# A hybrid encoder step: the second norm's product without GpSimd, the first FFN tiles feature by feature

## The chip, the cores and the metric

The kernel runs on one core of a Trainium2 chip. Such a core has five engines that work side by side, each through its own instructions in order: TensorE (PE, matmuls; PEld is its loading of weights), VectorE (DVE), ScalarE (ACT), GpSimd (POOL) and SyncE (SP, which here issues DMAs). The metric is the device time of one execution in microseconds, of the slowest core, here the only one. The kernel before takes 1071.52 us, the median of 3 runs (1070.22 to 1071.63).

## The reference, cut to what matters

One layer is applied to 512 prompt positions and to 32 sample positions, with 1024 features and an FFN of width 2816. The first half of the layer (first norm, input projection, attention, short convolution, gated merge) isn't touched by the change. From there on, for both streams:

```python
    x = x + gate1[:, None, :] * (merged @ w_out)

    h2 = modulate(rms_norm(x, g_norm2), shift2, scale2)      # xn * (1 + scale) + shift
    up, gate = jnp.split(h2 @ w_up, 2, axis=-1)
    up_c, new_ffn = causal_dwconv(up, ffn_prev, w_fconv, b_fconv)
    x = x + gate2[:, None, :] * ((jax.nn.silu(up_c) * gate) @ w_down)
```

The norm divides each position by the root of its mean square over the 1024 features. Shift, scale and gate are vectors over the features, one set for the prompt and one for the sample.

## The kernel before, in words

**Layout.** Features lie on the 128 partitions, in 8 tiles (KD = 8); the 544 positions are columns. They are cut into two halves of 272 columns (`HALF`), each of 256 prompt and 16 sample columns. As the modulation differs between prompt and sample, an operation that uses it is issued twice per half, on 256 and on 16 columns (`streams`, L662).

**Matmuls.** Each fp32 operand is split in a rounded part and the rest (`xh`, `xl`; `wh`, `wl`), and a product is three matmuls: `wh` with `xh`, `wh` with `xl`, `wl` with `xh` (`mm3_steps`, L105). One output tile of 128 features for one half is 8 features x 3 = 24 matmuls of 272 columns. The accumulators in PSUM rotate among three (`acc`, L121).

**The stretch of the change.** `w_out` has 8 output tiles. Tiles 0 to 3 are done for both halves at once. Tiles 4 to 7 ("late") are done for the first half in `out_half(0)` and then for the second in `out_half(1)` (L711). After each, `residual` (L667) adds the gated tile into `xr` on DVE, ACT squares it, and POOL adds the squares up in `sacc` for tiles 1 to 6 (L677); tile 0's squares start `sacc`, tile 7's stay in `sq2`. `norm` (L680) sums both over the features with matmuls against ones (`ss`), and `rstd_of` (L167) makes the inverse root `rs` from it: Ln and Exp on ACT, one Newton step on DVE (L171 to L176).

`h2` (L690) then makes the input of the FFN for one half, feature by feature (k = 0 to 7): POOL multiplies `xr` by `rs` into `hf` (L694; six buffers), DVE scales and shifts it, for prompt and sample apart (L697), and `split` (L89) has ACT round it to `h2h` (L91) and DVE subtract to get `h2l` (L92). The weights of the first FFN tiles, 0, KF = 22 (the gate of 0) and 1, are loaded ahead into the pool `early`, and `up_half(i)` (L718) computes these three tiles for one half, one tile after the other. From there the loop over `f` (L742) goes on: ACT copies the up tile out of its accumulator (L747), DVE convolves it, ACT applies silu (L750), DVE multiplies with the gate's accumulator (L754), and the result is split into `fh` and `fl`, which lie in memory that `early` and the pool of `mh` and `ml` have given back.

**What sets the order.** The instructions are written in program order, and a planner orders them for each engine: of those whose inputs are ready by its own model of durations, the one written first goes first. `tc.high_priority()` puts both calls of `norm` ahead of what was written before them. `after(inst, earlier)` (L154) makes the planner put `inst` behind `earlier` on their engine. In `h2` of the first half, features 5 to 7 are put so behind the last residual of `out_half(1)`.

Of the kernel before, what the change touches and what calls it, by code (L numbers as in the profile page):

```python
# [12 lines left out]
F32 = mybir.dt.float32  # L13
F32R = mybir.dt.float32r
AF = mybir.ActivationFunctionType
ALU = mybir.AluOpType
# [34 lines left out]
def build(tc, a):  # L51
    nc = tc.nc
    ctx = ExitStack()
    with ctx:
# [34 lines left out]
        def split(hi, lo, x, eng=nc.vector):  # L89

            nc.scalar.copy(hi, x)  # L91
            eng.tensor_tensor(lo, x, hi.bitcast(F32), ALU.subtract)  # L92

        def load_w(src, nk=KD, pool=wp, hl_bufs=2, lo=nc.vector):
            raw = wp.tile([P, KD, P], F32, tag="raw", bufs=4, name="raw")
            nc.sync.dma_start(raw[:, :nk], src)
            wh = pool.tile([P, KD, P], F32R, tag="wh", bufs=hl_bufs, name="wh")
            wl = pool.tile([P, KD, P], F32R, tag="wl", bufs=hl_bufs, name="wl")
            nc.scalar.copy(wh[:, :nk], raw[:, :nk])  # L99
            lo.tensor_tensor(wl[:, :nk], raw[:, :nk], wh[:, :nk].bitcast(F32), ALU.subtract)  # L100
            return wh, wl

        HALF = ((0, HT), (HT, T))

        def mm3_steps(ps, wh, wl, xh, xl, k0=0, nk=KD, first=True, last=True, cols=HALF):  # L105
            for k in range(nk):
                for w, xs in ((wh, (xh, xl)), (wl, (xh,))):
                    for n, x in enumerate(xs):
                        s = first and k == 0 and w is wh and n == 0
                        e = last and k == nk - 1 and w is wl  # L110
                        for i, (c0, c1) in enumerate(cols):
                            nc.tensor.matmul(ps[:, i, 0:c1 - c0], w[:, k], x[:, k0 + k, c0:c1], start=s, stop=e)  # L112
                yield

        def mm3(*args, **kw):
            for _ in mm3_steps(*args, **kw):
                pass
# [3 lines left out]
        def acc():  # L121
            acc_pools.rotate(-1)
            return acc_pools[-1].tile([P, 2, 512], F32, tag="mm", name="ps")[:, :, 0:HT]

        def proj(w, x):

            if not isinstance(w, tuple):
                w = load_w(w)
            ps = acc()
            mm3(ps, *w, *x)  # L130
            return ps
# [22 lines left out]
        def after(inst, earlier):  # L154

            tc.add_manual_dep(inst.ins, earlier.ins.name,
                              mybir.DependencyInfo(mybir.DependencyClass.NoSync, mybir.DependencyReason.DATA))
# [27 lines left out]
        mods = cp.tile([P, 6, KD, 2], F32, name="mods")  # L185
# [144 lines left out]
        for k in range(KD):  # L330
# [5 lines left out]
            hf = xt[:, k]  # L336
# [4 lines left out]
        for w, slot, post in zip(ws, slots, (queries, keys)):  # L341
            ps = slot[:, :, 0:HT]
# [56 lines left out]
        def transposed(sg):  # L399

            out = []
            for g in ROWS:
                at = pz.tile([P, 512], F32, tag="z", name="at")
                c = 0
                for i in g:
                    for b in range(i + 1):
                        s0 = SEG[b] + P * (i - b)
                        nc.tensor.transpose(at[:, c + P * b:c + P * b + P], sg[:, s0:s0 + P], ident)  # L408
                    c += P * (i + 1)
                ah = sp.tile([P, 512], F32R, tag="ah", bufs=3, name="ah")  # L410
                al = sp.tile([P, 512], F32R, tag="al", bufs=3, name="al")
                split(ah[:, :c], al[:, :c], at[:, :c])
                out.append((ah, al))
            return out
# [89 lines left out]
        earlier = None  # L504
        for j in range(NP):
            for e in range(2):
# [7 lines left out]
                earlier = (j, e, transposed(sg), vt)  # L514
# [112 lines left out]
        for b, w0, wb, br in ((0, 7 * KD, "w_branch_b", (bh, bl)), (1, 6 * KD, "w_branch_a", (oh, ol))):  # L627
# [7 lines left out]
            for m in range(KD):  # L635
                ps = proj(W[w0 + m], x)
                sg = mbp.tile([P, 2, HT], F32, tag="sg", bufs=2, name="sgm")
                last = nc.scalar.activation(sg, ps, AF.Sigmoid)
                ps = proj(load_w(a[wb][m], lo=nc.gpsimd), br)
# [15 lines left out]
        xr = xp.tile([P, KD, T], F32, name="xr")  # L655
# [3 lines left out]
        rs = xp.tile([P, T], F32, name="rs")  # L659
        sq2 = xp.tile([P, T], F32, name="sq2")  # L660

        def streams(c0, c1):  # L662

            e = c0 // HT * HT + HP
            return [(n, a_, b_) for n, a_, b_ in ((0, c0, min(c1, e)), (1, max(c0, e), c1)) if a_ < b_]

        def residual(ps, s, m, c0, c1):  # L667

            for n, a_, b_ in streams(c0, c1):
                r = xr[:, m, a_:b_]  # L670
                added = nc.vector.scalar_tensor_tensor(r, ps[:, a_ - c0:b_ - c0], mods[:, s, m, n:n + 1], r,
                                                       ALU.mult, ALU.add)
            sq = sacc[:, c0:c1] if m == 0 else sq2[:, c0:c1] if m == KD - 1 else \
                xp.tile([P, HT], F32, tag="sq", bufs=2, name="sq")
            nc.scalar.activation(sq, xr[:, m, c0:c1], AF.Square)  # L675
            if 0 < m < KD - 1:
                nc.gpsimd.tensor_tensor(sacc[:, c0:c1], sacc[:, c0:c1], sq, ALU.add)  # L677
            return added
# [8 lines left out]
        h2h = hp.tile([P, KD, T], F32R, tag="hh", name="h2h")  # L687
        h2l = hp.tile([P, KD, T], F32R, tag="hl", name="h2l")

        def h2(c0, c1, earlier=None):  # L690

            for k in range(KD):
                hf = xp.tile([P, HT], F32, tag="hf", bufs=6, name="hf2")
                nc.gpsimd.tensor_tensor(hf, xr[:, k, c0:c1], rs[:, c0:c1], ALU.mult)  # L694
                for n, a_, b_ in streams(c0, c1):
                    v = hf[:, a_ - c0:b_ - c0]
                    v = nc.vector.tensor_scalar(v, v, mods[:, 4, k, n:n + 1], mods[:, 3, k, n:n + 1], ALU.mult, ALU.add)  # L697
                    if earlier and k >= 5:
                        after(v, earlier)
                split(h2h[:, k, c0:c1], h2l[:, k, c0:c1], hf)  # L700

        tables = log_tables(last)
        wo = tc.alloc_tile_pool(name="wo", bufs=1)
# [1 line left out]
        for m in range(KD - NW):  # L705
            ps = proj(a["w_out"][m], (mh, ml))
# [2 lines left out]
        late = [(m, load_w(a["w_out"][m], pool=wo, hl_bufs=NW)) for m in range(KD - NW, KD)]  # L709

        def out_half(i):  # L711
            for m, w in late:
                ps = acc()[:, 0:1]
                mm3(ps, *w, mh, ml, cols=(HALF[i],))
                done = residual(ps[:, 0], 2, m, *HALF[i])
            return done

        def up_half(i):  # L718
            for w, ps in first.values():
                mm3(ps[:, i:i + 1], *w, h2h, h2l, cols=(HALF[i],))  # L720

        out_half(0)
        done = out_half(1)
        with tc.high_priority():
            norm(*HALF[0], tables, (sq2, sacc))
        h2(*HALF[0], done)
        first = {m: (load_w(a["w_up"][m], pool=early, hl_bufs=3), acc()) for m in (0, KF, 1)}
        with tc.high_priority():
            norm(*HALF[1], tables, (sq2, sacc))
        up_half(0)  # L730
        h2(*HALF[1])
        up_half(1)
        wo.release()
        ftp = ctx.enter_context(tc.tile_pool(name="ftmp", bufs=1))
# [7 lines left out]
        for f in range(KF):  # L742
            ps = first[f][1] if f in first else proj(a["w_up"][f], (h2h, h2l))
# [7 lines left out]
            ps = first[KF][1] if f == 0 else proj(a["w_up"][KF + f], (h2h, h2l))  # L751
# [7 lines left out]
        for m in range(KD - 1):  # L759
            ps = acc()  # L760
# [8 lines left out]
        m = KD - 1  # L769
# [7 lines left out]
        for c in HALF:  # L777
            ps = acc()[:, 0:1]
# [3 lines left out]
            cs = slice(*c)  # L782
# [74 lines left out]
```

## Time and profile before

| what | value |
|---|---|
| median of 3 runs | 1071.52 us |
| the profiled execution, own time | 1071.4 us |
| its span, from the first to the last instruction | 1069.7 us |
| PE busy | 1030.6 us (96%) |
| DVE busy | 616.0 us (58%) |
| ACT busy | 387.1 us (36%) |
| POOL busy | 164.9 us (15%) |
| mean granted TensorE clock | 0.990 |

Shares of busy time are averages over the whole span. The span is the time between the first and the last instruction of the profiled execution, and the execution's own time lies 1.7 us above it. A wait in the rows is written as "idle before", with the engine, tile and line that ended it.

### The profile page before, as it was taken

To read this page: it belongs to the slowest core of one execution; us is meant where nothing else is said; L and a number is where in the kernel's file an instruction comes from. 1 tells how busy PE (TensorE), PEld (TensorE's weight loads), DVE (VectorE), ACT (ScalarE), POOL (GpSimd) and SP (SyncE) were. 2 spreads that over 40 slices of the span, in tenths; PEclk is the share of its full clock that TensorE was granted. 3 is DMA by queue.
4 is the path that set the end of the run, shared out by engine and by line. 5 is a ranking of instruction groups with operands and counts; after the bars stand their busy time and mean duration, and the time that the engine had idled before them with its cause. 6 is when DMAs were issued, how large, how long until landed. Compare 5 with 4: busy or idle time off the path is not lost.

```text
span 1069.7 us, 19270 instructions
## 1 busy us (share of the span) xinstructions
PE 1030.6 (96%) x8042; PEld 1010.9 (95%) x8042; DVE 616.0 (58%) x914; ACT 387.1 (36%) x637; POOL 164.9 (15%) x247
## 2 busy tenths in 40 slices
PE   3899999999999999999999998999999999999995
PEld 1689999999999999999999997999999999999995
DVE  6956666656675556665777569454454545422234
ACT  5455544544443332222232443332323333332231
POOL 2520000000001112112111145000010001000112
PEclk9899999999999999999999999999999999999998
DMA  9636555554213225555555650123222222332312
GB/s 372 242 87 201 147 162 137 146 141 131 60 52 106 90 77 172 178 177 178 168 178 168 222 178 1 40 80 99 80 94 85 83 95 80 91 89 78 92 50 84
DMA packets 43271, 133.44 MB, mean 125 GB/s; under 512 B 5296, under 2 KB 8496, under 8 KB 43056
## 3 DMA queue, kind: packets, MB, share of 16 engines
q1 hardware_dynamic: 43040, 132.07, 39.1%
q8 instruction: 63, 1.03, 0.4%
q14 instruction: 24, 0.20, 0.1%
q10 hardware_dynamic: 144, 0.14, 0.1%
HBM read 112.60 MB, written 6.75 MB: 112 GB/s over the span
## 4 chain that ended last, share of the span: by engine, by line
PE 91%; DVE 5%; issue 1%; DMA 1%; ACT 1%; POOL 0%; SPq 0%; DVEq 0%; ACTq 0%; POOLq 0%
PE ps L112 83%; PE o L370 2%; PE z L370 2%; PE at L408 2%; DVE hf L697 1%; DVE adum L196 1%; PE slot L112 1%; DMA cbc<-in_c_dram 1%; PE mt L315 1%; DVE h2l L92 1%; DVE xt L337 0%; SPq L289 0%; PE so L370 0%; PE tp L268 0%; POOL hl L92 0%
## 5 line engine op out<-in xcount | busy, mean ns | idle before, releaser
L99 ACT CAST wh<-raw 128x1024 fp32r<-128x1024 f32 x153 | 159.1, 1041 | 362.3 <-PE ps L112 269.0
L100 DVE TENSOR_TENSOR wl<-raw,wh 128x1024 fp32r<-128x1024 f32 (+1 forms) x133 | 161.1, 1214 | 189.8 <-ACT wh L99 189.1
L112 PE MATMUL ps<-hh,wh 128*128 128x272 f32 x992 | 209.1, 291 | 0.0
L112 PE MATMUL ps<-hh,wl 128*128 128x272 f32 x992 | 205.4, 288 | 0.0
L112 PE MATMUL ps<-hl,wh 128*128 128x272 f32 x992 | 205.1, 288 | 0.0
L112 PEld LDWEIGHTS ps<-hh,wh 128*128 128x128 f32 x992 | 155.8, 188 | 1.6 <-issue 0.5
L112 PEld LDWEIGHTS ps<-hl,wh 128*128 128x128 f32 x992 | 155.8, 188 | 0.0
L112 PEld LDWEIGHTS ps<-hh,wl 128*128 128x128 f32 x992 | 155.3, 189 | 0.0
L112 PE MATMUL ps<-h2h,wh 128*128 128x272 f32 x704 | 150.5, 289 | 1.0 <-ACT h2h L91 1.0
L112 PE MATMUL ps<-h2l,wh 128*128 128x272 f32 x704 | 150.2, 289 | 1.2 <-DVE h2l L92 1.1
L112 PE MATMUL ps<-h2h,wl 128*128 128x272 f32 x704 | 150.4, 290 | 0.0
L112 PEld LDWEIGHTS ps<-h2l,wh 128*128 128x128 f32 x704 | 112.8, 189 | 2.1 <-DVE h2l L92 2.1
L112 PEld LDWEIGHTS ps<-h2h,wh 128*128 128x128 f32 x704 | 112.8, 189 | 1.9 <-ACT h2h L91 1.9
L112 PEld LDWEIGHTS ps<-h2h,wl 128*128 128x128 f32 x704 | 112.1, 190 | 0.0
L196 DVE SCALAR_TENSOR_TENSOR adum<-araw,cbc 128x1024 f32<-128x1024 f32 x64 | 82.7, 1292 | 41.2 <-DMA araw<-in_w_ada_dram 40.5
L100 POOL TENSOR_TENSOR wl<-raw,wh 128x1024 fp32r<-128x1024 f32 x20 | 50.0, 2501 | 170.5 <-ACT wh L99 160.9
L112 PE MATMUL ps<-fh,wh 128*128 128x272 f32 x308 | 63.6, 288 | 0.0
L112 PE MATMUL ps<-fl,wh 128*128 128x272 f32 x308 | 63.5, 288 | 0.0
L112 PE MATMUL ps<-fh,wl 128*128 128x272 f32 x308 | 63.4, 287 | 0.0
L394 DVE TENSOR_TENSOR_SCAN keep<-keep,whole 128x384 f32<-128x384 f32 (+1 forms) x48 | 46.7, 1029 | 18.7 <-ACT keep L392 18.7
L677 POOL TENSOR_TENSOR sacc<-sacc,sq 128x272 f32<-128x272 f32 x24 | 28.8, 1217 | 141.5 <-ACT sq L675 141.4
L112 PEld LDWEIGHTS ps<-fl,wh 128*128 128x128 f32 x308 | 48.4, 188 | 0.0
(197 smaller groups left out, 1536.2 us busy)
## 6 DMA issues: line engine op xcount, KB each, us to landing
raw<-in_w_in_dram SPq DMA_DIRECT2D x64, 512.0 KB, 3.7
raw<-in_w_up_dram SPq DMA_DIRECT2D x44, 512.0 KB, 3.4
araw<-in_w_ada_dram SPq DMA_DIRECT2D x32, 512.0 KB, 3.6
kt<-ko SPq DMA_DIRECT2D x32, 256.0 KB, 4.9
raw<-in_w_down_dram SPq DMA_DIRECT2D x16, 512.0 KB, 3.5
mraw<-in_w_ada_dram SPq DMA_DIRECT2D x10, 512.0 KB, 7.1
qt<-qo SPq DMA_DIRECT2D x32, 136.0 KB, 3.0
raw<-in_w_branch_b_dram SPq DMA_DIRECT2D x8, 512.0 KB, 3.4
```

Source lines behind the costliest of these rows:

```text
L92: eng.tensor_tensor(lo, x, hi.bitcast(F32), ALU.subtract)
L99: nc.scalar.copy(wh[:, :nk], raw[:, :nk])
L100: lo.tensor_tensor(wl[:, :nk], raw[:, :nk], wh[:, :nk].bitcast(F32), ALU.subtract)
L112: nc.tensor.matmul(ps[:, i, 0:c1 - c0], w[:, k], x[:, k0 + k, c0:c1], start=s, stop=e)
L196: nc.vector.scalar_tensor_tensor(adum, raw, 1.0, cbc[:, n], ALU.mult, ALU.mult, accum_out=sums[:, n:n + 1])
L315: nc.tensor.matmul(rows, sct[:, i], raw[:, i * P:i * P + P], start=i == 0, stop=i == KD - 1, skip_group_check=True)
L370: nc.tensor.matmul(out, l, r, start=s, stop=t, skip_group_check=True)
L394: nc.vector.tensor_tensor_scan(kb, kb, whole[:, m0:m0 + c], 1.0, ALU.mult, ALU.max)
L408: nc.tensor.transpose(at[:, c + P * b:c + P * b + P], sg[:, s0:s0 + P], ident)
L677: nc.gpsimd.tensor_tensor(sacc[:, c0:c1], sacc[:, c0:c1], sq, ALU.add)
L697: v = nc.vector.tensor_scalar(v, v, mods[:, 4, k, n:n + 1], mods[:, 3, k, n:n + 1], ALU.mult, ALU.add)
```

## The change

`h2` no longer uses POOL. One DVE operation per stream makes `xr` times the scale times `rs`; ACT adds the shift while it rounds to `h2h`; and DVE adds the shift and subtracts `h2h` in one operation per stream to get `h2l`. `out_half` returns the last residual additions of tiles 5, 6 and 7 in place of that of tile 7 alone, and in the first half the prompt's products are put behind them: feature 1 and all later ones behind tile 5's, feature 3 and later behind tile 6's, feature 5 and later behind tile 7's. `up_half` computes its three tiles in turns, all three for feature 0, then all three for feature 1, and so on.

```diff
-        def h2(c0, c1, earlier=None):
+        def h2(c0, c1, earlier=()):
             for k in range(KD):
                 hf = xp.tile([P, HT], F32, tag="hf", bufs=6, name="hf2")
-                nc.gpsimd.tensor_tensor(hf, xr[:, k, c0:c1], rs[:, c0:c1], ALU.mult)
                 for n, a_, b_ in streams(c0, c1):
+                    cs = slice(a_, b_)
                     v = hf[:, a_ - c0:b_ - c0]
-                    v = nc.vector.tensor_scalar(v, v, mods[:, 4, k, n:n + 1], mods[:, 3, k, n:n + 1], ALU.mult, ALU.add)
-                    if earlier and k >= 5:
-                        after(v, earlier)
-                split(h2h[:, k, c0:c1], h2l[:, k, c0:c1], hf)
+                    i = nc.vector.scalar_tensor_tensor(v, xr[:, k, cs], mods[:, 4, k, n:n + 1], rs[:, cs], ALU.mult, ALU.mult)
+                    for first_k, add in zip((1, 3, 5), earlier):
+                        if k >= first_k and n == 0:
+                            after(i, add)
+                for n, a_, b_ in streams(c0, c1):
+                    cs = slice(a_, b_)
+                    v, shift = hf[:, a_ - c0:b_ - c0], mods[:, 3, k, n:n + 1]
+                    nc.scalar.activation(h2h[:, k, cs], v, AF.Identity, bias=shift)
+                    nc.vector.scalar_tensor_tensor(h2l[:, k, cs], v, shift, h2h[:, k, cs].bitcast(F32), ALU.add, ALU.subtract)
...
         def out_half(i):
+            done = []
             for m, w in late:
                 ps = acc()[:, 0:1]
                 mm3(ps, *w, mh, ml, cols=(HALF[i],))
-                done = residual(ps[:, 0], 2, m, *HALF[i])
-            return done
+                done.append(residual(ps[:, 0], 2, m, *HALF[i]))
+            return done[1:]

         def up_half(i):
-            for w, ps in first.values():
-                mm3(ps[:, i:i + 1], *w, h2h, h2l, cols=(HALF[i],))
+            for _ in zip(*[mm3_steps(ps[:, i:i + 1], *w, h2h, h2l, cols=(HALF[i],)) for w, ps in first.values()]):
+                pass
```

## Rows read from the trace of the kernel before

**Rows 1.** The page's head: the span, and each engine's busy us, share and instructions.

```profile
span 1069.7 us, 19270 instructions
PE 1030.6 (96%) x8042; PEld 1010.9 (95%) x8042; DVE 616.0 (58%) x914; ACT 387.1 (36%) x637; POOL 164.9 (15%) x247
```

**Rows 2.** The chain that ended last: start us, us, engine, tile, line.

```profile
648.75 0.54 DVE xr L671 x2
...
662.94 0.70 DVE h2l L92 x2
...
668.88 379.08 PE ps L112 x3012
```

**Rows 3.** PE in order of time: start us, us, line, shapes [idle before].

```profile
650.58 0.29 PE L112 MATMUL ps<-h2h,wh 128*128 128x272 f32 x1
...
654.24 0.73 PE L684 MATMUL ssh<-sq,ones 128*128 128x272 f32 x2 [1.77 <-ACT sq L675]
...
655.06 0.49 PE L112 MATMUL ps<-h2h,wl 128*128 128x272 f32 x1
...
666.07 0.39 PE L112 MATMUL ps<-h2l,wh 128*128 128x272 f32 x1 [0.81 <-DVE h2l L92]
```

**Rows 4.** DVE in order of time, merged.

```profile
642.28 0.43 DVE L176 SCALAR_TENSOR_TENSOR rs<-nt,rs 128x272 f32<-128x272 f32 x1
...
643.60 3.87 DVE L697 TENSOR_SCALAR hf<-hf,mods 128x256 f32<-128x256 f32 x5 [0.74 <-POOL hf L694]
...
653.10 0.62 DVE L671 SCALAR_TENSOR_TENSOR xr<-ps,mods,xr 128x256 f32<-128x256 f32 x2
653.64 1.74 DVE L697 TENSOR_SCALAR hf<-hf,mods 128x256 f32<-128x256 f32 x5
...
657.72 0.44 DVE L176 SCALAR_TENSOR_TENSOR rs<-nt,rs 128x272 f32<-128x272 f32 x1
...
674.72 0.79 DVE L754 TENSOR_TENSOR gf<-ps,fcv 128x512 f32<-128x512 f32 x2 [0.91 <-PE ps L112]
```

**Rows 5.** ACT in order of time, merged: the first FFN tile.

```profile
670.89 0.67 ACT L747 COPY up<-ps 128x512 f32<-128x512 f32 x2 [1.55 <-PE ps L112]
671.58 1.28 ACT L750 ACT_TABLE_LOAD   x1
...
677.67 0.65 ACT L91 CAST fh<-gf 128x544 fp32r<-128x544 f32 x1 [3.17 <-PE ps L112]
```

**Rows 6.** Windows: stretch, its length, each engine's busy us, clock, DMA.

```profile
650.58:663.25 12.67, 10.77 (x78) 9.95 (x77) 11.73 (x30) 4.57 (x11) 5.89 (x10) 1.00 0.01 3
663.25:669.40 6.15, 4.08 (x22) 2.73 (x20) 6.05 (x19) 2.51 (x6) 1.62 (x2) 0.96 0.00 0
669.40:672.40 3.00, 3.00 (x14) 3.00 (x14) 1.18 (x3) 1.49 (x3) 0.31 (x2) 0.50 0.00 0
```

**Rows 7.** Groups by line and shape: count | busy us, mean ns | idle before.

```profile
L787 DVE SCALAR_TENSOR_TENSOR xr<-xr,vec,rs 128x272 f32<-128x272 f32 x2 | 1.0, 490 | 0.0
L671 DVE SCALAR_TENSOR_TENSOR xr<-ps,mods,xr 128x256 f32<-128x256 f32 x16 | 7.6, 478 | 7.6 <-PE ps L112 7.5
L671 DVE SCALAR_TENSOR_TENSOR xr<-ps,mods,xr 128x16 f32<-128x16 f32 x16 | 3.6, 224 | 0.0
L339 ACT ACTIVATE xt<-xt,mods 128x512 f32<-128x512 f32 x8 | 6.5, 815 | 0.9 <-DVE xt L337 0.5
L339 ACT ACTIVATE xt<-xt,mods 128x32 f32<-128x32 f32 x8 | 3.2, 398 | 0.0
```

**Rows 8.** ACT in order of time, in the first norm.

```profile
16.17 0.66 ACT L172 ACTIVATE y<-nt 128x544 f32<-128x544 f32 x1
16.73 0.37 ACT L325 ACTIVATE mods<-sums,b1g,vec 128x2 f32<-128x2 f32 x1
```

## The prediction

> **What bounds the kernel now.** The page's summary comes first. TensorE (PE) is busy for 1030.6 of 1069.7 us, GpSimd (POOL) for 164.9 [rows 1]: the kernel is a stream of matmuls, and a change helps only where that stream has holes. Next the chain that ended last: around the second norm it leaves PE for VectorE (DVE), and from 668.88 on it is one unbroken PE piece of 379.08 us with 3012 matmuls, 0.126 us each [rows 2]. So whatever is won before 668.88 moves all that follows one for one, unless a new hole opens; that piece has no slack in which it could vanish.
>
> Then I priced the holes on PE's timeline. The first matmul of `up_half(0)` starts at 650.58 [rows 3]. `up_half(0)` and `up_half(1)` need 3 tiles x 2 halves x 24 = 144 matmuls, 18.1 us, and the norm's sums for the second half stand among them, from 654.24 to 655.06, 0.8 us [rows 3]. Without holes the three tiles would be finished at 650.58 + 18.9 = 669.5. They are finished at 677.5: DVE's product with tile KF, which waited for that tile, starts at 674.72 [rows 4]; tile 1 has 24 matmuls more, 3.0 us; and the cast of `fh` on ScalarE (ACT), which takes over the memory of the three tiles' weights, waited for PE until 677.67 [rows 5]. **8.0 us are lost here.** The reader sees the pieces: 1.8 us before the norm's sums, 0.8 us before the h2l at 666.07 [rows 3], and then the granted clock of 0.50, the 1.2 GHz level, from 669.4 to 672.4, after a stretch in which PE was busy for 4.08 of 6.15 us [rows 6]. The 3.0 us at that level hold some 13 matmuls, worth 1.6 us at the other: 1.4 us of the eight.
>
> Why the holes: DVE is busy for 11.73 of 12.67 us and for 6.05 of 6.15 in these stretches [rows 6], so PE waits for DVE. Five scalings `hf` take 3.87 us, 0.77 each, where POOL multiplies for the next features, and a later five 1.74 (wide and narrow ones are merged in these rows) [rows 4]. The residual is late too: PE is done with tile 7 of `out_half(1)` at 650.6, but DVE adds it at 653.10 [rows 4], and its square on ACT is what the norm's sums wait for [rows 3]. And `up_half` runs tile by tile: tile 0 asks for all eight features within 3.0 us.
>
> **Part 1: the product without GpSimd.** Removed are, per feature and half, one multiplication on POOL and three operations on DVE (two scalings, one subtraction). Added: four operations on DVE, two of 256 columns and two of 16, all with two tensors and a column of scalars, and on ACT two additions of the shift for one cast. No DMA is issued, removed or moved, so the queues of SP and POOL stay.
>
> The neighbours of the DVE operations have the same opcode: 490 ns for 272 columns out of SBUF, 478 and 224 ns for 256 and 16 columns in the residual [rows 7]. A residual's pair 256 + 16 takes 0.54 us on the chain, where consecutive operations overlap [rows 2]. Upper bound per feature: no overlap, 2 x (0.49 + 0.22) = 1.42 us; lower bound: two subtractions of 272 columns take 0.70 [rows 2], so 0.70 if the narrow ones were free. I take 2 x 0.54 = 1.08, as the residual's pair has this very form.
> For ACT the nearest rows are 815 ns for 512 columns and 398 for 32, with two columns of scalars [rows 7]: 0.87 ns per column, so 0.59 + 0.38 = 0.97 us per feature as the upper bound, and the `fh` cast's 0.65 for 544 columns [rows 5] as the lower. ACT is busy for 4.57 of 12.67 us there [rows 6], and 0.97 is still under DVE's 1.08, so DVE hides it.
>
> A rule of the Trainium skill speaks against this part. "VectorE: DVE Perf Modes", section on the perf-mode tier table, gives a one-tensor fp32 operation, which is what the scalings are, twice the rate of a two-tensor one; by the formula (N+151)/0.96 on that page the four new operations take an estimated 1.20 us. The trace does not show the fast form run fast: 0.77 us beside POOL [rows 4]. By 1.20, DVE would end at 666.4 in the walk below, still before PE wants the last feature, so the sum is the same by rule and by row.
>
> **Part 2: the order on DVE.** The products of the first half may now be only one feature ahead of the residual of tile 5, three of tile 6, five of tile 7. That adds waits on DVE, which works in order: behind them stand later features, which PE reads no sooner than 650.58. The walk: rs is there at 642.7 [rows 4]. Feature 0 ends at 643.9. PE ends tiles 5, 6 and 7 at 644.6, 647.6 and 650.6 (24 matmuls each). Residual 5 ends at 645.2, features 1 and 2 at 647.3, residual 6 at 648.2, features 3 and 4 at 650.3, residual 7 at 651.4, its square at 651.9 instead of 654.2. The sums follow (0.8), and from their end to rs it is as before, 655.06 to 658.16, 3.1 us [rows 3, 4]: rs of the second half at 655.8. Features 5 to 7 (3.2) and the norm's four operations (some 1.8) fill DVE from 651.4 to 656.4, and the second half's eight are done at 656.4 + 8.6 = 665.0.
>
> **Part 3: feature by feature.** PE now reads one feature for 9 matmuls, 1.13 us, against 1.08 in which DVE makes one. It wants the first half's feature 5 at 650.6 + 0.8 + 5.7 = 657.1 (ready by 653.5), the second half's feature 0 at 660.4 (ready near 658.2) and its feature 7 at 668.3 (ready at 665.0): it is not starved. At the upper bound of 1.42 DVE ends at 651.4 + 1.8 + 11 x 1.42 = 668.8, and PE waits half a microsecond; at the lower bound nothing is gained, as PE sets the pace.
> The weaving uncovers two things. Three accumulators rotate, and tile 1 takes the one of tile 7 of `out_half(1)`: wanted some 6 us after 650.58 before, now at 651.3, and free when residual 7 has read it, 651.4 or one DVE operation later: 0.1 to 0.5 us, up to 1.2 if PE stands there for the norm's sums too. I take 0.4. And all three tiles now end together: the next one, KF+1, takes the accumulator of tile 0, which ACT's two copies free in 0.67 us [rows 5]. Before, they ran 6 us before it was wanted; now tile 0 ends only 6 matmuls, 0.75 us, ahead, so 0 to 0.7 us remain, and I take 0.2. After these copies come convolution, table load (1.28 [rows 5]), silu and product, 670.89 to 675.5, 4.6 us [rows 4, 5], until tile KF's accumulator is free; it is wanted 6.0 us (48 matmuls) later: hidden, with more than a microsecond over.
>
> **The sum.** 8.0 (holes and low clock) - 0.4 - 0.2 = 7.4 us gained. The profiled run took 1071.4 (its span 1069.7), so 1064.0; the median of the runs shown, 1071.52, lies 0.1 above it, so 1064.1.
>
> **Rivals.**
> (a) Half. The norm's sums are put on PE well behind residual 7, as they were (14 matmuls after 650.58), and more: 4.2 us later than in my walk use up the 2.2 us by which feature 0 of the second half is early, and PE waits 2.0; with both new waits at their ends, 1.2 + 0.7, the loss is 3.9, the gain 4.1: 1067.4. For it: PE's order is the planner's, made with its own durations. Against: residual 7 no longer stands behind the last features.
> (b) Moved: the gain is lost behind 669.5, because accumulator KF comes free late, or fh's memory. More than a microsecond of cover would have to go, and then 6 us besides: 1071.
> (c) Slower: DVE makes each feature in series: product 0.49 + 0.22, ACT 0.97, difference 0.49 + 0.22, and nothing of another feature between them, 2.39 us. DVE ends at 653.2 + 11 x 2.39 = 679.5, PE has 9 matmuls left at the low clock (2.0): 681.5 against 677.5, 1075.5. It decides from about 2.0 us a feature, where 653.2 + 11 x 2.0 + 2.0 reaches 677.5. Against: DVE does five scalings before it turns to the first h2l [rows 4], and there are six `hf` buffers as before.
> (d) That Identity makes ACT reload its table, 1.28 us each time: in the first norm an Identity (L325) follows Exp (L172) with no load between them [rows 8], so this gets no chance of its own.
>
> **Chances.** Forecast 0.74, half 0.14, moved 0.07, slower 0.05. A measurement of this kernel tells about 0.2%, 2.1 us, from no change. Faster by more: 0.74 + 0.14 = 0.88; within: 0.07; slower: 0.05. The forecast's own range is 1063.0 (nothing lost, and half a microsecond from an order that shifts elsewhere) to 1065.5 (both waits at their ends). For 8 in 10 I take 1062.8 to 1067.0, most of the way to (a).
>
> **What would show it.** Right: between 650 and 671 PE has no hole above 0.6 us and a granted clock of 1.00; tile KF+1 starts near 670.1; residual 7 starts on DVE before 651.3; DVE's features come about 1.1 us apart; POOL is left with the sums of squares. Wrong: PE waits for h2l feature after feature and the 0.50 comes back, a wait for ACT's `up` copies above 0.7 us opens the FFN, or PE's unbroken piece after it has holes.

## The result, and the profile after

The changed kernel takes 1063.62 us, the median of 5 runs (1063.5 to 1064.93), where five runs of the kernel before on the same chip had a median of 1071.52. The ratio is 0.994, with a 95% interval of 0.9926 to 0.9954. The prediction said 1064.1.

The head of the page after, in the columns of [rows 1]:

```profile
span 1061.4 us, 19274 instructions
PE 1024.2 (96%) x8042; PEld 1007.8 (95%) x8042; DVE 612.8 (58%) x930; ACT 391.6 (37%) x653; POOL 151.2 (14%) x231
```

POOL has lost the 16 multiplications and DVE has gained 16 instructions, as the diff says. PE is busy for 6.4 us less with the same count. Only 2.9 of these lie behind the first matmul of `up_half(0)` (393.25 us busy before, 390.31 after, up to the final norm): what was lost there was not only idle time but slow matmuls too. The other 3.5 lie ahead of it, where nothing was edited.

The chain that ended last, after, from residual 7 on, as the residual addition of tile 7 in `out_half(1)` is called from here on (start us, us, engine, tile, line):

```profile
649.74 0.55 DVE xr L671 x2
650.28 0.14 issue
650.42 0.74 PE ps L112 x4
651.16 0.92 PE ssh L684 x4
652.07 16.70 PE ps L112 x133
668.78 0.01 issue
668.79 371.09 PE ps L112 x2958
```

In [rows 2] the chain went through DVE at 648.75 and at 662.94, and the unbroken PE piece began at 668.88, inside `up_half(1)`. Now it leaves DVE with the residual of tile 7, and from 650.42 to the final norm PE has one stop of 0.01 us, at 668.78, where tile KF+1 begins.

PE in order of time, after: the only hole in these three tiles, the norm's sums, and then PEld at the start of tile KF+1 (columns of [rows 3]):

```profile
650.42 0.36 PE L112 MATMUL ps<-h2h,wh 128*128 128x272 f32 x1 [0.40 <-DVE xr L671]
...
651.00 0.62 PE L684 MATMUL ssh<-sq,ones 128*128 128x272 f32 x2
...
668.78 0.30 PEld L112 LDWEIGHTS ps<-h2h,wh 128*128 128x128 f32 x2 [0.23 <-ACT up L754]
```

The holes of 1.77 and 0.81 us in [rows 3] are gone. The two waits that stand are the two that the prediction had priced at 0.4 and 0.2.

DVE in order of time, after (columns of [rows 4]):

```profile
649.65 0.62 DVE L671 SCALAR_TENSOR_TENSOR xr<-ps,mods,xr 128x256 f32<-128x256 f32 x2
...
654.32 0.44 DVE L176 SCALAR_TENSOR_TENSOR rs<-nt,rs 128x272 f32<-128x272 f32 x1
654.79 1.17 DVE L697 SCALAR_TENSOR_TENSOR hf<-xr,mods,rs 128x256 f32<-128x256 f32 x4
...
663.29 0.63 DVE L705 SCALAR_TENSOR_TENSOR h2l<-hf,mods,h2h 128x256 fp32r<-128x256 f32 x2 [0.29 <-ACT h2h L704]
```

The first matmul of `up_half(0)` stands at 648.99. Residual 7 starts 0.66 us after it (2.52 before, [rows 3, 4]), the second half's `rs` is ready 5.8 us after it (7.6 before), and its eight features take from 654.79 to 663.92, 1.14 us each.

Windows, after: the stretch from the first matmul of `up_half(0)` to that of tile KF+1, and five microseconds of its middle (stretch, length, busy us of PE, PEld, DVE, ACT and POOL, clock, DMA share, GB/s):

```profile
648.99:668.79 19.80, 19.39 (x151) 18.83 (x149) 14.58 (x52) 9.52 (x28) 0.37 (x3) 1.00 0.00 1
653.00:658.00 5.00, 5.00 (x42) 5.00 (x41) 4.93 (x18) 2.38 (x8) 0.00 (x0) 1.00 0.01 3
```

The clock is 1.00 all through; the 0.50 of [rows 6] does not come. DVE is still busy for nearly all of the middle, but PE no longer waits for it.

**Where the 8.3 us between the two spans are.** I count 148 instructions of PE (144 matmuls and 4 sums) from the first matmul of `up_half(0)` to that of tile KF+1: 26.89 us before, 19.80 after, so 7.09 come from the stretch. Another 1.59 come from the profiled run of after reaching that stretch sooner (648.99 against 650.58). PE's work up to there was not edited, and over the thirteen profiled kernels that start lies between 648.24 and 651.58, in no order that follows the edits (650.58 before, 650.50 and 648.24 in two kernels without a hole behind it); I don't count it to the change. From KF+1 to the final norm's first sums PE needs 370.92 instead of 370.33, 0.59 lost, and the tail gives 0.21. To compare kernels without the moving start, I use the time from the first matmul of `up_half(0)` to the final norm's first sums, called **rest** below: 397.22 before, 390.72 after, 6.50 less. The ratio's interval, 4.9 to 7.9 us, holds it. Each rest is read from one trace.

### The profile page after: what moved, and what is told of

Its sections match the earlier page's. It is cut to its first block, busy times and chain, and to the rows that moved or that the text cites. A ratio compares the mean times of both kernels' runs of the same rounds, so it can differ in the third digit from the quotient of the medians.

```text
span 1061.4 us, 19274 instructions
## 1 busy us (share of the span) xinstructions
PE 1024.2 (96%) x8042; PEld 1007.8 (95%) x8042; DVE 612.8 (58%) x930; ACT 391.6 (37%) x653; POOL 151.2 (14%) x231
## 4 chain that ended last, share of the span: by engine, by line
PE 92%; DVE 4%; DMA 2%; issue 1%; ACT 1%; POOL 0%; DVEq 0%; SPq 0%; ACTq 0%; POOLq 0%
PE ps L112 85%; PE o L370 2%; PE z L370 2%; PE at L408 2%; DVE adum L196 2%; DMA cbc<-in_c_dram 1%; DMA ks<-in_cache_k_dram 1%; PE slot L112 0%; PE ssh L684 0%; PE so L370 0%; PE tp L268 0%; DMA vec<-in_vec_dram 0%; DMA mraw<-in_w_shift_dram 0%; DVE hf L697 0%; DVE h2l L705 0%
## 5 line engine op out<-in xcount | busy, mean ns | idle before, releaser
L112 PEld LDWEIGHTS ps<-fh,wh 128*128 128x128 f32 x308 | 48.3, 188 | 0.0
```

## Experiments

The prediction read three parts as one gain. The first theory (A) followed it: the order on DVE and the feature by feature order on PE carry the gain, and leaving GpSimd is worth little, since DVE gets four operations per feature for three. The rival (B): GpSimd's multiplications slow DVE's operations beside them, and leaving GpSimd is the whole gain. Each ratio below is against runs of the kernel before on the same chip. Computing the three tiles in turns, feature by feature, is called weaving.

**The old h2 with only the weaving of PE's tiles** (the kernel before, with the loop of `up_half` alone changed):

```diff
-            for w, ps in first.values():
-                mm3(ps[:, i:i + 1], *w, h2h, h2l, cols=(HALF[i],))
+            for _ in zip(*[mm3_steps(...) for w, ps in first.values()]):
+                pass
```

> The kernel before with one part alone: the three first FFN tiles feature by feature; product on GpSimd and old order on DVE stay. Stretch = first matmul of up_half(0) to first matmul of tile KF+1 (27.0 us before, 19.8 after). Theory (PE starves because a tile asks for eight features in 3.0 us, and the residual of tile 7 is late): weaving removes the first, the second stays and now holds tile 1's accumulator: a wait of about 2.4 us at 651.3, none at the second half (its last h2l ends at 669.8, wanted at 670.6). Stretch 21.5 us, 1066 us. Rival (GpSimd's product beside DVE is the whole cause, the order of the tiles nothing): stretch stays above 25, 1070 or more.

Measured: 1066.29 us, ratio 0.9966 (0.9956 to 0.9977), rest 393.31. So weaving does win 3.9 us while GpSimd multiplies, near what A expected, and PE's granted clock is 1.00 from 648 to 670. What is left is mainly a hole for the accumulator of tile 7:

```profile
653.24 0.36 PE L112 MATMUL ps<-h2h,wh 128*128 128x272 f32 x1 [1.73 <-DVE xr L671]
```

Weaving puts tile 1 right behind the start, and so makes PE depend on residual 7 at once.

**Only the product without GpSimd** (the changed kernel with the order and the tiles of before):

```diff
-                    for first_k, add in zip((1, 3, 5), earlier):
-                        if k >= first_k and n == 0:
-                            after(i, add)
+                    if earlier and k >= 5:
+                        after(i, earlier[-1])
...
+            for w, ps in first.values():
+                mm3(ps[:, i:i + 1], *w, h2h, h2l, cols=(HALF[i],))
```

> The kernel after with two parts undone: tiles one after the other, and features 5 to 7 alone behind the residual of tile 7; only the product without GpSimd is left. Theory: features come every 1.1 us, tile 0 asks for them every 0.38, so PE waits about 1.8 us in the first half and 0.2 to 1 in the second; the residual of tile 7 is in time, as five features of 1.1 and three residuals end before PE does. Stretch 21 to 22 us, 1065.5 to 1066.5. Rival (GpSimd is the whole cause): stretch near 19.5, 1063.5 or less, as the waits for accumulators go too. Second rival (without the new order the residual stays late): stretch 23.5 or more, 1068.

Measured: 1063.28 us, ratio 0.9938 (0.9922 to 0.9954), rest 389.97. This is all of the gain and a little more, as B had it and A had not. The chain from 640 to 700 is PE alone:

```profile
639.92 9.85 PE ps L112 x78
649.77 1.12 PE ssh L684 x4
650.89 49.11 PE ps L112 x388
```

PE has no hole at all in the rest, and residual 7 starts 0.34 us after the first matmul, without the new order.

**The order and the weaving, with GpSimd kept** (the kernel before with both other parts of the diff):

```diff
-                    if earlier and k >= 5:
-                        after(v, earlier)
+                    for first_k, add in zip((1, 3, 5), earlier):
+                        if k >= first_k and n == 0:
+                            after(v, add)
...
-                done = residual(ps[:, 0], 2, m, *HALF[i])
-            return done
+                done.append(residual(ps[:, 0], 2, m, *HALF[i]))
+            return done[1:]
```

> The kernel after with one part undone: GpSimd makes the product again and DVE scales and shifts as before; new order on DVE and weaving stay. Theory: the residual of tile 7 is in time, the sums end near 652.7, the second half's features come every 1.35 to 1.45 us from 656 on and end near 667.6, where PE wants the last at 668.3: no wait, stretch 19.6 to 20.5 us, 1063.5 to 1064.5; the part without GpSimd is then worth next to nothing by itself. Rival (GpSimd beside DVE is the cause): PE waits feature by feature, stretch 23 or more, 1067 or more.

Measured: 1070.92 us, ratio 1.0005 (0.9993 to 1.0017), rest 396.51. Here theory A fell. DVE in order of time (columns of [rows 4]):

```profile
643.91 3.69 DVE L697 TENSOR_SCALAR hf<-hf,mods 128x256 f32<-128x256 f32 x5 [0.73 <-POOL hf L694]
...
647.88 1.48 DVE L697 TENSOR_SCALAR hf<-hf,mods 128x16 f32<-128x16 f32 x2
649.27 0.61 DVE L671 SCALAR_TENSOR_TENSOR xr<-ps,mods,xr 128x256 f32<-128x256 f32 x2
...
655.50 0.61 DVE L671 SCALAR_TENSOR_TENSOR xr<-ps,mods,xr 128x256 f32<-128x256 f32 x2
```

The first matmul stands at 650.95, so residual 7 starts 4.55 us after it, later than the 2.52 of before. The new order holds back the prompt's products (`n == 0`); the 16-column scalings of later features are free of it, and six of them go ahead of the residual of tile 5, at 649.27. Beside GpSimd each takes 0.72 to 0.82 us (two of them the 1.48 us above). PE then waits for `xr` twice, 2.16 us at 653.65 and 1.88 at 656.26.

**Without GpSimd, the new order, tiles one after the other** (the changed kernel with the `up_half` of before):

```diff
+            for w, ps in first.values():
+                mm3(ps[:, i:i + 1], *w, h2h, h2l, cols=(HALF[i],))
```

> The kernel after with one part undone: the three tiles one after the other again. Theory: the two accumulator waits (0.7 us together) go, but tile 0 waits for features 5 to 7 in the first half (1.5 us) and for the last ones in the second (1.0): stretch 18.9 + 2.5 = 21.4 us, 1065.2 us. Rival (weaving is no cause): stretch 19.2, 1063.0.

Measured: 1063.0 us, ratio 0.994 (0.9924 to 0.9956), rest 390.20. PE idles 0.24 us, ahead of the sums. With GpSimd gone, weaving adds nothing.

**The changed kernel with GpSimd multiplying again, unread.** Nothing is left out; per feature the old multiplication is added into a tile that nobody reads:

```diff
+                idle = xp.tile([P, HT], F32, tag="idle", bufs=1, name="idle")
+                nc.gpsimd.tensor_tensor(idle, xr[:, k, c0:c1], rs[:, c0:c1], ALU.mult)
```

> The kernel after, and beside it GpSimd again multiplies all 16 features' halves, into a tile that nobody reads; PE's order is that of after. Rest = first matmul of up_half(0) to the final norm's first sums: before 397.2, after 390.7, p1_only 390.0, p2p3_pool 396.5, p3_only 393.3, p1p2_tiles 390.2 us. New theory (while GpSimd's two-tensor operation runs, a DVE operation waits for it, wide or narrow, so DVE, which works in order, falls behind the order planned for it): 8 multiplications of 0.78 us per half hold DVE for some 4 us per half, the residuals of tiles 5 to 7 come 2 to 4 us late, tile 1 waits for its accumulator: rest 393 to 396 us, 1066 to 1069 us, and operations of 256 columns take 0.7 us or more beside GpSimd. Rival (it was the step through GpSimd in the chain, a latency, and not its presence): rest 390.7, 1063.6.

Measured: 1070.45 us, ratio 1.0002 (0.9991 to 1.0013), rest 396.38, both above the ranges expected. Nothing reads what is added and PE's order is the same, yet the whole gain is gone: theory B is shown. GpSimd and then PE's holes, in order of time:

```profile
643.68 5.21 POOL L695 TENSOR_TENSOR idle<-xr,rs 128x272 f32<-128x272 f32 x6
```

```profile
651.05 0.36 PE L112 MATMUL ps<-h2h,wh 128*128 128x272 f32 x1 [1.51 <-DVE xr L671]
...
654.29 0.37 PE L112 MATMUL ps<-h2h,wh 128*128 128x272 f32 x1 [2.50 <-DVE xr L671]
```

DVE's groups by shape over 643.6 to 649.7 of this kernel, and then over 643.1 to 649.6 of the changed one (count | busy us, mean ns):

```profile
L707 DVE SCALAR_TENSOR_TENSOR h2l<-hf,mods,h2h 128x256 fp32r<-128x256 f32 x3 | 3.0, 1021 | 0.0
L699 DVE SCALAR_TENSOR_TENSOR hf<-xr,mods,rs 128x16 f32<-128x16 f32 x3 | 1.7, 591 | 0.0
L699 DVE SCALAR_TENSOR_TENSOR hf<-xr,mods,rs 128x256 f32<-128x256 f32 x2 | 1.4, 748 | 0.0
L707 DVE SCALAR_TENSOR_TENSOR h2l<-hf,mods,h2h 128x16 fp32r<-128x16 f32 x2 | 0.9, 480 | 0.0
L671 DVE SCALAR_TENSOR_TENSOR xr<-ps,mods,xr 128x256 f32<-128x256 f32 x1 | 0.5, 471 | 0.0
```

```profile
L697 DVE SCALAR_TENSOR_TENSOR hf<-xr,mods,rs 128x16 f32<-128x16 f32 x4 | 1.8, 495 | 0.0
L705 DVE SCALAR_TENSOR_TENSOR h2l<-hf,mods,h2h 128x256 fp32r<-128x256 f32 x4 | 1.7, 476 | 0.0
L697 DVE SCALAR_TENSOR_TENSOR hf<-xr,mods,rs 128x256 f32<-128x256 f32 x4 | 1.7, 471 | 0.0
L705 DVE SCALAR_TENSOR_TENSOR h2l<-hf,mods,h2h 128x16 fp32r<-128x16 f32 x5 | 1.0, 225 | 0.0
L671 DVE SCALAR_TENSOR_TENSOR xr<-ps,mods,xr 128x256 f32<-128x256 f32 x2 | 0.9, 472 | 0.0
```

In the mean the same instruction takes 1021 in place of 476 ns, or 748 in place of 471, and the narrow ones wait as well (480 for 225). These means mix operations that wait with some that don't: in the first kernel the single products of 256 columns took 501 and 995, the narrow `h2l` 740 and 221. In the changed kernel the 495 of the narrow products comes from GpSimd's sums of squares, which are still there: two of the four took 766 and 768, the others some 225. The residual, one of whose inputs lies in PSUM, takes 471 or 472 either way. The Trainium skill, "SBUF — State Buffer", section "Who interferes with whom", has the rule: a DVE instruction with two inputs from SBUF contends with a GpSimd instruction that reads SBUF, and one with at most one such input, outside the two-port modes, does not. These two traces agree with it, in both halves.

**One word of the kernel before:**

```diff
-                nc.gpsimd.tensor_tensor(hf, xr[:, k, c0:c1], rs[:, c0:c1], ALU.mult)
+                nc.vector.tensor_tensor(hf, xr[:, k, c0:c1], rs[:, c0:c1], ALU.mult)
```

> The kernel before with one word changed: the product of xr and rs on DVE in place of GpSimd, nothing else (scaling, cast, subtraction, order and tiles as before). DVE gets a fourth operation per feature, 1.2 us in all. New theory (GpSimd's presence is the cause): nearly all of the gain is there, rest 390 to 391.5 us, 1063 to 1064.5 us. Rival (the fused operations and the shift on ACT are needed, as DVE has too much to do): rest 393 or more, 1066 or more.

Measured: 1065.36 us, ratio 0.995 (0.9934 to 0.9966), rest 390.67: the rest as expected, the time 0.9 us above its range. DVE now does one operation more per feature than before, and 6.55 of the 7.25 us between before and the kernel without holes are won. Fusing the product with the scale and giving the shift to ACT, with no other part, add the other 0.7. DVE's scalings here, from 643 to 664 (the means hold one of each width that ran beside a sum of squares, 909 and 747 ns; the others take 399 to 405 and 277 to 291), and in the first experiment, where GpSimd multiplies beside them, from 643 to 650:

```profile
L697 DVE TENSOR_SCALAR hf<-hf,mods 128x256 f32<-128x256 f32 x14 | 6.1, 438 | 0.0
...
L697 DVE TENSOR_SCALAR hf<-hf,mods 128x16 f32<-128x16 f32 x14 | 4.4, 316 | 0.0
```

```profile
L697 DVE TENSOR_SCALAR hf<-hf,mods 128x256 f32<-128x256 f32 x4 | 3.6, 898 | 0.7 <-POOL hf L694 0.7
L697 DVE TENSOR_SCALAR hf<-hf,mods 128x16 f32<-128x16 f32 x3 | 1.8, 589 | 0.0
```

**Only the product, PE held to program order.** In the run with only the product the planner had itself woven tiles 0 and KF (after the sums: 8 matmuls of tile 0, 4 of KF, 2, 4, 1, 7 ...; in the kernel before, in the first half, only 6 of KF stand ahead of the last 2 of tile 0). This kernel forbids it: the first matmul of each tile is put behind the last of the tile ahead (`made` collects a tile's matmuls):

```diff
+                made = []
+                mm3(ps[:, i:i + 1], *w, h2h, h2l, cols=(HALF[i],), made=made)
+                if up_last:
+                    after(made[0], up_last.pop())
+                up_last.append(made[-1])
```

> p1_only with PE held to the order of the program: each of the three tiles starts behind the last matmul of the one ahead of it, in both halves; DVE and ACT as in p1_only. There the planner wove two of the tiles by itself. Theory (a tile asks for eight features in 3.0 us, and weaving, by whomever, hides that): PE waits 2.2 us in the first half for features 5 to 7 and up to 0.4 in the second: rest 392 to 393 us, 1065 to 1067 us. Rival (with GpSimd gone features come early enough for any order): rest 390.0, 1063.3.

Measured: 1064.69 us, ratio 0.9949 (0.9932 to 0.9966), rest 391.62, 1.65 us more than without the bond; less than expected. PE's three holes:

```profile
655.15 0.39 PE L112 MATMUL ps<-h2l,wh 128*128 128x272 f32 x1 [0.27 <-DVE h2l L706]
656.14 0.39 PE L112 MATMUL ps<-h2h,wh 128*128 128x272 f32 x1 [0.47 <-ACT h2h L705]
657.04 0.39 PE L112 MATMUL ps<-h2l,wh 128*128 128x272 f32 x1 [0.51 <-DVE h2l L706]
```

So tile by tile does starve PE, as the prediction said, but of 7 us only this much, and left to itself the planner's order avoids it.

**Without GpSimd, woven, in the old order** (the changed kernel with the order of before):

```diff
-                    for first_k, add in zip((1, 3, 5), earlier):
-                        if k >= first_k and n == 0:
-                            after(i, add)
+                    if earlier and k >= 5:
+                        after(i, earlier[-1])
```

> The kernel after with one part undone: only features 5 to 7 stand behind the residual of tile 7, as in before; no GpSimd, woven. PE's order is that of after. New theory: without GpSimd beside it DVE ends five features and three residuals before PE ends tile 7, so the order by parts gains nothing: rest 390.5 to 390.9 us, 1063.5 us. Rival (the order on DVE carries part of the gain): residual of tile 7 over 1 us later than in after (where it starts 0.66 us after the first matmul of up_half(0)), rest 392 or more, 1065 or more.

Measured: 1064.62 us, ratio 0.9944 (0.9928 to 0.9959), rest 389.97, a little below the range expected (the time is 1.1 us above it). Residual 7 starts 0.41 us after the first matmul and PE waits once, 0.15 us, so the new order is not what makes it early.

**Only the new order**, GpSimd kept, tiles one after the other (the diff of the third experiment without the weaving):

```diff
-                        after(v, earlier)
+                            after(v, add)
```

> The kernel before with one part alone: the products of the first half ordered by parts behind the residuals of tiles 5, 6 and 7; GpSimd's product and the tiles one after the other stay. New theory: the order does not bring the residual forward beside GpSimd (in p2p3_pool tile 7's started 4.6 us after the first matmul of up_half(0), in before 2.5), so PE waits longer for the norm's sums: rest 397 to 399 us, 1071 to 1073 us. Rival (the order by itself brings the residual forward, and weaving spoilt it in p2p3_pool): rest 395 or less, 1069 or less.

Measured: 1073.82 us, ratio 1.0025 (1.0014 to 1.0037), rest 398.73, in the range expected, the time 0.8 us above its own. Alone this part costs 1.5 us: residual 7 starts 4.56 us after the first matmul.

**A smaller dose:** the unread multiplications only for the first four features of each half.

```diff
+                if k < 4:
+                    idle = xp.tile([P, HT], F32, tag="idle", bufs=1, name="idle")
+                    nc.gpsimd.tensor_tensor(idle, xr[:, k, c0:c1], rs[:, c0:c1], ALU.mult)
```

> pool_noise with half the dose: GpSimd multiplies for features 0 to 3 of each half only, into a tile that nobody reads. New theory: 8 multiplications in the first half made the residual of tile 7 3.9 us later than in after, 0.5 us each, so 4 make it 1.9 us later; PE then waits about 1.9 us more than in after for tile 1's accumulator, and the second half has slack for its four: rest 392.6 to 393.5 us, 1065.5 to 1066.5 us. Rival (a threshold: beside any GpSimd work the order breaks): rest near 396. Second rival (DVE catches up before tile 7): rest 390.7.

Measured: 1066.55 us, ratio 0.9969 (0.9955 to 0.9983), rest 394.36, more than expected. Residual 7 is 2.27 us later than in the changed kernel, 0.57 for each of four multiplications, and PE's hole is 2.51 instead of 0.40. Behind the hole the granted clock falls (windows, as above):

```profile
656.00:659.00 3.00, 3.00 (x14) 2.79 (x13) 3.00 (x11) 2.12 (x7) 0.00 (x0) 0.59 0.00 0
```

14 matmuls in the 3.00 us, where 24 fit at the other level: 1.2 us. Hole and clock together are 3.3 of the 3.64 us.

**Another operation on GpSimd:** an unread copy of `rs`, 487 ns, in place of the unread multiplication, 840 ns.

```diff
+                nc.gpsimd.tensor_copy(idle, rs[:, c0:c1])
```

> pool_noise with a copy (one tensor read) in place of each GpSimd multiplication (two read), 16 of them, into a tile that nobody reads. If a DVE operation waits for any GpSimd operation, DVE loses for as long as the copies last: in proportion to their duration, rest 392 to 396 us, and wide DVE operations beside them take 0.7 us or more. If only two-tensor operations collide, DVE's keep 0.47 us and rest stays near 390.7 us, 1063.6 us.

Measured: 1065.7 us, ratio 0.9953 (0.9937 to 0.9968), rest 391.88. The rest falls below the first range and above the second figure. Copies delay DVE too, but less: the products of 256 columns take 529 ns in place of 476, those of 16 columns 374 in place of 294 (means over all sixteen features), and PE has one hole of 1.73. One product of 256 columns beside a multiplication, in the kernel with all sixteen, and one beside a copy, here:

```profile
646.29 0.83 POOL L695 TENSOR_TENSOR idle<-xr,rs 128x272 f32<-128x272 f32 x1
646.41 0.99 DVE L699 SCALAR_TENSOR_TENSOR hf<-xr,mods,rs 128x256 f32<-128x256 f32 x1
```

```profile
644.59 0.49 POOL L695 COPY idle<-rs 128x272 f32<-128x272 f32 x1
644.72 0.63 DVE L699 SCALAR_TENSOR_TENSOR hf<-xr,mods,rs 128x256 f32<-128x256 f32 x1
```

Both products end 0.27 to 0.28 us after GpSimd's operation. So the copy, which reads one tensor, holds DVE up to its end as the multiplication does, and costs less because it is shorter.

**The three parts side by side.** All eight combinations ran; rest in us, and the start of residual 7 after the first matmul:

| product | order on DVE | tiles | rest | residual 7 |
|---|---|---|---|---|
| GpSimd | old | one after the other (before) | 397.22 | 2.52 |
| GpSimd | new | one after the other | 398.73 | 4.56 |
| GpSimd | old | woven | 393.31 | 2.48 |
| GpSimd | new | woven | 396.51 | 4.55 |
| DVE | old | one after the other | 389.97 | 0.34 |
| DVE | new | one after the other | 390.20 | 0.65 |
| DVE | old | woven | 389.97 | 0.41 |
| DVE | new | woven (after) | 390.72 | 0.66 |

With GpSimd the order costs 1.5 to 3.2 us and weaving wins 2.2 to 3.9. Without it neither moves the rest by more than 0.8. The four kernels with the product on DVE differ by less than their timed intervals; by the traces one of each, the new order and the weaving together are 0.75 worse than the product alone.

## Why the prediction was right, and where it was not

**The time** came out 0.5 us from the forecast, in part by luck, as the next two paragraphs show. What the changed kernel was to show came out as well: the clock of 1.00, the two small waits at 0.40 and 0.2, residual 7 early, a feature every 1.14 us (1.08 predicted), 19.80 us for the stretch. No rival occurred: in this stretch PE waits neither for `h2l` nor, beyond 0.23, for ACT's copies. (Rival (a) counts 14 matmuls ahead of the sums before; the trace has 11, before and after.)

**The first term was 0.8 too large.** 8.0 us were to be lost before 669.5. The kernels without a hole need 389.97 for the rest, so before loses 7.25: PE is busy for 393.25 of its 397.22 us with the same 3108 records, which makes 3.97 of idle time and 3.28 of slow matmuls. In the two kernels that need 389.97, the stretch takes 19.54 and 19.65 us, not 18.9; the four sums, which I had at 0.8, take 0.92 and 1.12 on PE in the chains above, and that is a part of it. So the change was worth 6.5 in the rest, where I had 7.4; the start of the profiled run, 1.59 us sooner by chance, hides that in the spans.

**The step that failed is the cause.** "Why the holes" named five scalings at 0.77 each "where POOL multiplies for the next features" beside a later five at 1.74 us in all, and then went on as if that were a property of the scalings: Part 1 compared counts of operations and found DVE no worse off, Part 2 had the new order bring residual 7 forward, and Part 3 had the tiles' order end the starving. The runs put it otherwise. A DVE operation of `h2` that is caught by GpSimd's multiplication ends only after it, about 0.5 us late; DVE, which works in order, falls behind; the residuals that stand behind those operations come late, and so the sums of the norm, `rs`, and all features of the second half. Taking the multiplication away heals all of this, and then neither order moves the rest by more than 0.8. By the prediction's attribution the third experiment should have taken 1063.5 to 1064.5 us; it took 1070.92. That PE's order counts on shorter durations of DVE is argued: no run shows the planner's own figures.

**What Part 2 missed** is what stands behind its own waits: products of 256 columns held behind a residual let narrow operations of later features pass, and beside GpSimd these took 0.72 to 0.82 each, six of them ahead of the residual of tile 5.

**The rule on the scalings' rate** changed nothing in the sum, as the prediction had it: 1.14 us a feature is above the 1.08 taken from the residual's pair. By the Trainium skill, "VectorE: DVE Perf Modes", section on the perf-mode tier table, the scalings of before should have twice the rate of two-tensor operations; the estimate of 1.20 us came from a formula of the same page of the skill. The 0.77 us beside POOL could not test that; with GpSimd away the trace agrees, per column: undisturbed scalings take some 402 ns for 256 columns and 284 for 16, 0.49 ns a column, where the two-tensor product takes 474 and 224, 1.04 a column. The scalings' larger fixed part hides most of it at this size.

**Left open:** why the long PE piece takes 0.59 us more, 370.92 against 370.33. It is 370.32 in the run with the product alone, 370.43 woven in the old order, and 370.92 in the two woven kernels with GpSimd; no row shows a wait in it. The starts of its matmuls show where it lies: 0.10 right behind the first matmul of tile KF+1, in every woven kernel, and 0.51 spread evenly over the 989 matmuls of `w_down` up to the final norm's first sums (124.03 us after, 123.52 before).

## What to carry to other kernels

Work that is given to GpSimd need not be free for DVE: look for the same DVE operation at two durations in one trace, and at what GpSimd does beside the slow one, before counting operations. The delay spreads through the order: price not the slow operation but the instruction behind it on its engine, and who waits for that. When a change has several parts, a forecast of the sum that comes true says nothing on the parts; run each alone.

## What the runs showed of the hardware that was not expected

Operations of 16 columns lose about as much beside GpSimd as those of 256. In the kernel with the unread multiplications, the narrow ones that waited took 736 to 806 ns where the others took some 225, the wide ones 981 to 1108 where the others took some 474: 0.5 to 0.6 us each. The residual, with one input in PSUM, loses nothing (471 against 472). One-tensor scalings lose too: those of 256 columns take 840 to 935 ns in the kernel before where they are caught by a multiplication, some 402 undisturbed. Against the rule cited above, one input from SBUF is then no protection, unless the scalings run in the two-port modes that it excepts; no run separates that.

GpSimd can be the one that loses. In the run that moves the product to DVE, a sum of squares that starts at 650.47, 0.02 us after a DVE product, takes 2.08 us in place of 0.77, while DVE's two-tensor operations beside it keep their 428 to 430 ns.
